# Loading, splitting and summing one half of the output's left operands from the fourth tile of mixer A's branch on

## The chip, the cores and the metric

The kernel runs on one core of a Trainium2 chip. The metric is the device time of one execution in microseconds (us), as the median of several runs. The engines are named PE (TensorE, matrix products), DVE (VectorE), ACT (ScalarE), POOL (GpSimd) and SP (SyncE, which here only issues transfers); PEld is the loading of weights into PE. A DMA is a transfer between the chip's memory and the core's SBUF.

## The reference

One layer of a decoder block on a sequence of 1024 rows and a width of 1024. Three branches (mixer A, a chunked spatial gating; mixer B, a windowed attention; mixer M, an attention into a memory) are each projected back to width 1024, summed under sigmoid gates, and multiplied by one output matrix:

```python
u = jax.nn.gelu(a_u, approximate=False)
vv = layer_norm(jax.nn.gelu(a_v, approximate=False), a_v_norm_w, a_v_norm_b)
y_a = chunked_spatial_gating(u, vv, a_spatial_w, a_spatial_b) * jax.nn.silu(a_z)
...
merged = (gates[:, :, 0] * (y_a @ proj_a)
          + gates[:, :, 1] * (y_b @ proj_b)
          + gates[:, :, 2] * (y_m @ proj_m))
x = x + merged @ w_out
```

The change touches how `merged @ w_out` is prepared while `y_a @ proj_a` is still being computed.

## The kernel before

**Number format.** A float32 operand is split into a high and a low part (`split`, L137 on ACT makes the high one, L138 on DVE the low one), and each product is three matrix products (`mm3`, L159 to L161). `piece` loads a weight (`ws_`, L142) and splits it into `wh_` and `wl_`.

**The stage around the change.** The last gating stage is mixer A's branch: `gates(0, w_pa, 6, yas, (0, 4, 1, 5, 2, 6, 3, 7), merged_done)`. It goes through eight tiles `dt` of the output's channels in that order, and each tile has two halves of 512 rows (tile 7 does its second half first). A half is one group of 18 matrix products (six weights of 128 columns, three products each) into one PSUM bank `pp`. PSUM has four banks of the tag `pj`, so the group that comes four later can only begin when DVE has read the bank at L1204 (`tg = (tg + 1) * pp`). Then POOL issues at L1206 a DMA that adds `tg` into `merged[dt]`; in tile 7 DVE adds it itself at L1208. The gate `tg` of a tile is loaded by SP at L1183 into one of three places.

**The output product** is done by a scheme of seven products over quadrants of the operands. Its right operands are `ro` (`right_sums`): for each pair of tiles `dt - 4` and `dt` it forms sums of quadrants of `merged` (L1301, L1305, L1306, L1307 on DVE) and splits each into two halves (`half_split`: L1288 on ACT, L1289 on DVE). L1301 needs both halves of `merged[dt - 4]` with the added `tg`, L1305 the second half of `merged[dt]`.

Its left operands are `left_o`, pieces of `w_out` for two column halves `c` and two row halves `kh`. For each (`c`, `kh`) `left_o_steps` gives the steps: "load" (four quadrants of 128x512), 1 to 7 (split for product 1 to 7), "sums" (L341 makes `so` from quadrants 21 and 22; L342 and L343 then combine quadrant 11 with them), and "last" (L346). The raw quadrants of `kh == 0` are in the weights' places `ws_o`, shared by all weights; those of `kh == 1` are in four places `wr_o` of their own (L1323).

**What sets the order.** The order in which the code is written is not that of the engines' queues: a scheduler lets the program's steps run ahead (so loads that the code asks for in tile 3 stand several tiles earlier on SP). Each engine runs its own queue strictly in order and stops at an instruction whose inputs aren't there.

After the stage, `partial(c, j, n, ks)` computes the products `po`, whose banks come from the same `pj` places (products 2 and 3 excepted); the first four begin with three of their four weights' tiles.

Of the kernel before, what the change touches and what calls it, by code (L numbers as in the profile page):

```python
# [41 lines left out]
def hybrid_block(  # L42
# [130 lines left out]
    last = [None]  # L173
# [156 lines left out]
    def prepare_left(load, extra, ready):  # L330


        w = {}

        def loads(*blocks):
            for b in blocks:
                w[b] = load((11, 21, 22, 12).index(b))

        def sums():
            w["s"] = extra()  # L340
            V.tensor_tensor(out=w["s"], in0=w[21], in1=w[22], op=ALU.add)  # L341
            V.tensor_tensor(out=w[21], in0=w[11], in1=w[21], op=ALU.subtract)  # L342
            V.tensor_tensor(out=w[11], in0=w["s"], in1=w[11], op=ALU.subtract)  # L343

        def last():
            V.tensor_tensor(out=w[12], in0=w[12], in1=w[11], op=ALU.subtract)  # L346

        return {"load": lambda: loads(11, 12, 21, 22), "11": lambda: loads(11), "12": lambda: loads(12),
                "2": lambda: loads(21, 22), "sums": sums, "last": last,
                1: lambda: ready(w[11], 1), 2: lambda: ready(w[12], 2), 3: lambda: ready(w[12], 3), 4: lambda: ready(w[22], 4), 5: lambda: ready(w["s"], 5),  # L350
                6: lambda: ready(w[11], 6), 7: lambda: ready(w[21], 7)}

# [22 lines left out]
    steps = deque()  # L375
# [7 lines left out]
    def ready(name):  # L383
        return lambda st, q: prepared.append(parts(st, 512, f"{name}_{q}"))
# [3 lines left out]
    def add_steps(ps_):  # L388


        def step(*keys):
            def run():
                for key in keys:
                    for p in ahead[nxt] if isinstance(key, tuple) and nxt < len(ahead) else ps_:
                        if not isinstance(key, tuple):
                            p[key]()
                        elif nxt < len(ahead):
                            for k in key if len(ahead[nxt]) == 2 else ("load",) * (key == ("2",)):
                                p[k]()
            return run  # L400

        n = len(ps_)
        ahead.append(ps_)
        nxt = len(ahead)
        steps.extend((n, step(*keys)) for keys in ((1,), (2,), ("sums", 6), (7, ("11",)), (5,), (4, ("12",)),
                                                   ("last", 3, ("2",))))

    tstack = ExitStack()
# [454 lines left out]
    with tc.tile_pool(name="npool", reuse_waits="tile", bufs=1, side="right") as npool:  # L863
# [55 lines left out]
        for b, targets in enumerate(naturals):  # L919
# [48 lines left out]
            for q in range(7):  # L968
                w = take(2)
                rh, rl = rights[q]  # L970
                for t in range(2):
# [13 lines left out]
                    n = len(later)  # L985
# [27 lines left out]
    with tc.tile_pool(name="ppool", reuse_waits="tile", bufs=1, side="right") as pp_:  # L1013
# [49 lines left out]
        for i, kind in enumerate(pairs):  # L1063
# [8 lines left out]
            for q in range(7):  # L1072
                p = 7 * i + q
# [210 lines left out]
    osteps = {}  # L1284
# [52 lines left out]
    def next_steps(c, n):  # L1337

        for p in osteps[c]:
            for key in ((1,), ("sums", 5), (2, "last", 3), (), (6,), (7,), (4,))[n]:  # L1340
                p[key]()

    def begin(c):
        osteps[c] = [left_o_steps(c, kh) for kh in range(2)]
        for p in osteps[c]:
            p["load"]()
        next_steps(c, 0)

    def merged_done(dt):
        right_sums(dt)  # L1350
        if dt == 3:
            begin(0)
            next_steps(0, 1)

    gates(0, w_pa, 6, yas, (0, 4, 1, 5, 2, 6, 3, 7), merged_done)
    next_steps(0, 2)
    late = deque(sorted(late, key=lambda t: PORDER.index(t[0])))
    jobs = [(0, j, n) for js in ((0, 1), (2, 3)) for ns in (range(2), range(2, 7)) for j in js for n in ns]
# [20 lines left out]
    for c, j, n in jobs:  # L1379
# [16 lines left out]
        if (c, j) == (0, 3):  # L1396
            if n == 0:
                begin(1)
            elif n != 2:
                next_steps(1, 2 if n == 3 else n)  # L1400

        def vadd(o, b=acc):
            V.tensor_tensor(out=o, in0=b, in1=o, op=ALU.add)
# [113 lines left out]
```

## Time and profile before

| what | value |
|---|---|
| three runs | 1119.02, 1120.58 and 1123.42 us |
| their median | 1120.58 us |
| the profiled execution's own time | 1120.26 us |
| the span of its trace | 1118.5 us |
| PE busy | 98 % of the span |
| DVE busy | 71 % |
| ACT busy | 46 % |
| POOL busy | 17 % |

The times in the rows below are microseconds from the beginning of the span of the profiled execution. Its own time, taken from outside, is 1.76 us longer than the span. The stage of mixer A's branch that the change touches runs from about 957 to 1024 us, and the output product follows it to the end.

### The profile page before, as it was taken

How to read it: one execution, taken by the hardware profiler on the slowest of the kernel's cores; microseconds unless marked ns; L12 is line 12 of the kernel's file. 1: busy time of each engine (PE TensorE's matmuls, PEld its weight loads, DVE VectorE, ACT ScalarE, POOL GpSimd, SP SyncE). 2: the span in 40 equal slices, each digit the busy share in tenths (PEclk: the TensorE clock that was granted, in tenths of full speed). 3: DMA queues.
4: the chain of work that ended last, by engine and by line, in shares of the span. 5: the costliest groups of instructions: out<-in, count | busy, mean ns of one | idle time of the engine just before them, and what ended most of it. 6: DMA issues, size and time to landing. Idle time of an engine off the chain costs nothing.

```text
span 1118.5 us, 18302 instructions
## 1 busy us (share of the span) xinstructions
PE 1092.7 (98%) x6680; PEld 955.9 (85%) x6680; DVE 794.1 (71%) x1701; ACT 514.0 (46%) x1123; POOL 195.7 (17%) x250
## 2 busy tenths in 40 slices
PE   8989999999999999999999999999999999998998
PEld 7879999999988887888888888888888787886998
DVE  6999899856687766656555656687885467568863
ACT  6553333223245543755665554666564562134320
POOL 0000431321000002011111111111111026511232
PEclk9999999999999999999999999999999999999999
DMA  7222322454242423444434325455544975665432
GB/s 236 76 96 91 128 86 96 144 190 151 72 142 94 129 98 119 143 147 153 128 121 136 124 95 181 123 180 157 166 132 132 335 273 160 173 161 136 142 107 83
DMA packets 84558, 157.57 MB, mean 141 GB/s; under 512 B 9605, under 2 KB 30708, under 8 KB 84468
## 3 DMA queue, kind: packets, MB, share of 16 engines
q1 hardware_dynamic: 68164, 106.87, 30.6%
q0 software_dynamic: 14864, 47.05, 13.0%
q10 hardware_dynamic: 1440, 2.49, 0.6%
q8 instruction: 52, 0.85, 0.3%
q14 instruction: 38, 0.31, 0.1%
HBM read 106.84 MB, written 48.22 MB: 139 GB/s over the span
## 4 chain that ended last, share of the span: by engine, by line
PE 86%; DVE 5%; DMA 4%; issue 3%; POOL 1%; ACT 1%; SPq 0%; POOLq 0%; DVEq 0%; ACTq 0%
PE t L159 12%; PE t L161 12%; PE t L160 11%; PE n L160 7%; PE n L159 7%; PE n L161 7%; PE po L606 3%; PE pp L159 2%; DMA merged<-tg 2%; PE pp L161 2%; PE pp L160 2%; PE po L160 2%; PE po L159 2%; PE po L161 2%; PE pt L599 1%
## 5 line engine op out<-in xcount | busy, mean ns | idle before, releaser
L159 PE MATMUL t<-th,wh_t 128*128 128x512 f32 x336 | 135.2, 402 | 0.0
L161 PE MATMUL t<-th,wl_t 128*128 128x512 f32 x336 | 132.0, 393 | 0.0
L160 PE MATMUL t<-tl,wh_t 128*128 128x512 f32 x336 | 131.4, 391 | 0.0
L159 PE MATMUL n<-wh_n,th 128*128 128x256 f32 x384 | 108.2, 282 | 0.0
L161 PE MATMUL n<-wh_n,tl 128*128 128x256 f32 x384 | 107.6, 280 | 0.0
L160 PE MATMUL n<-wl_n,th 128*128 128x256 f32 x384 | 107.6, 280 | 0.0
L161 PEld LDWEIGHTS t<-th,wl_t 128*128 128x128 f32 x336 | 63.1, 188 | 14.5
L159 PEld LDWEIGHTS n<-wh_n,th 128*128 128x128 f32 x384 | 73.3, 191 | 1.5 <-issue 0.9
L160 PEld LDWEIGHTS t<-tl,wh_t 128*128 128x128 f32 x336 | 63.3, 188 | 12.8
L159 PEld LDWEIGHTS t<-th,wh_t 128*128 128x128 f32 x336 | 63.3, 188 | 12.3
L160 PEld LDWEIGHTS n<-wl_n,th 128*128 128x128 f32 x384 | 72.1, 188 | 0.2 <-issue 0.2
L161 PEld LDWEIGHTS n<-wh_n,tl 128*128 128x128 f32 x384 | 72.2, 188 | 0.0
L159 PE MATMUL t<-H2h,wh_t 128*128 128x512 f32 x168 | 67.8, 404 | 0.0
L137 ACT CAST wh_t<-ws_t 128x512 fp32r<-128x512 f32 x86 | 51.8, 619 | 33.3 <-PE n L161 11.8
L161 PE MATMUL t<-H2h,wl_t 128*128 128x512 f32 x168 | 65.9, 392 | 0.0
L160 PE MATMUL t<-H2l,wh_t 128*128 128x512 f32 x168 | 65.5, 390 | 0.0
L138 DVE TENSOR_TENSOR wl_t<-ws_t,wh_t 128x512 fp32r<-128x512 f32 x86 | 58.2, 685 | 10.0 <-ACT wh_t L137 9.9
L1069 DVE TENSOR_TENSOR o<-t,sa 128x512 f32<-128x512 f32 x63 | 43.3, 687 | 29.5 <-PE t L161 25.1
L1038 POOL DMA_DIRECT2D scr_g<-o x48 | 26.1, 544 | 191.9 <-ACT o L1024 167.1
L939 POOL TENSOR_TENSOR on<-on,nss 128x1024 f32<-128x1024 f32 x12 | 26.2, 2205 | 173.4 <-DVE nss L134 116.0
L159 PE MATMUL n<-wh_n,H2h 128*128 128x256 f32 x192 | 54.9, 286 | 0.1
L160 PE MATMUL n<-wl_n,H2h 128*128 128x256 f32 x192 | 54.3, 283 | 0.0
(382 smaller groups left out, 3185.1 us busy)
## 6 DMA issues: line engine op xcount, KB each, us to landing
ws_t<-in_w_t SPq DMA_DIRECT2D x64, 256.0 KB, 3.5
scr_g<-o POOLq DMA_DIRECT2D x48, 256.0 KB, 2.7
tg<-scr_g SPq DMA_DIRECT2D x16, 512.0 KB, 3.9
ws_n<-in_w_n SPq DMA_DIRECT2D x24, 256.0 KB, 3.3
wr_n<-in_w_n SPq DMA_DIRECT2D x24, 256.0 KB, 3.3
scr_qk<-on POOLq DMA_DIRECT2D x12, 512.0 KB, 4.3
bx<-scr_qk SPq DMA_DIRECT2D x24, 256.0 KB, 3.3
wr_t<-in_w_t SPq DMA_DIRECT2D x20, 256.0 KB, 3.5
```

The lines of the kernel that those rows point to most:

```text
L137: A.copy(out=hi, in_=y)
L138: (eng or V).tensor_tensor(out=lo, in0=y, in1=hi.bitcast(F32), op=ALU.subtract)
L159: T.matmul(o, lhsT=ah, rhs=bh, start=first, stop=False)
L160: T.matmul(o, lhsT=ah, rhs=bl, start=False, stop=False)
L161: T.matmul(o, lhsT=al, rhs=bh, start=False, stop=last)
L599: T.transpose(p2[:, h * P:(h + 1) * P], c.pr[h // 2][:, h % 2, b * P:(b + 1) * P], ident)
L606: T.matmul(po[:, 64 * h:64 * h + 64], lhsT=c.pT[b][:, h * P:(h + 1) * P], rhs=mb.v[:, (t - nk + 1 + b) % 3, 64 * h:64 * h + 64], start=b = ...
L939: G.tensor_tensor(out=v, in0=v, in1=ss[:, 16 * ORD[q]:16 * ORD[q] + 16].unsqueeze(2) .to_broadcast([P, 16, 64]), op=ALU.mult)
L1038: G.dma_start(out=t[:, h], in_=d)
L1069: V.tensor_tensor(out=o[q], in0=psum, in1=s, op=ALU.add)
```

## The change

The combining steps of a left operand, which were one step "sums", become two: "s" (L341) and "rest" (L342 and L343, in the changed kernel L344 and L345). For the first column half (`c == 0`) the two row halves no longer go together: `kh == 1` is loaded and split for product 1 after the fourth tile (`dt == 5`) of mixer A's branch, gets its "s" and the split for product 5 after the fifth, and its "rest" after the sixth. `kh == 0` keeps its place after the seventh tile (`dt == 3`), but its "rest" comes behind the whole stage. For `c == 1` "rest" is done behind the split for product 5. The number of instructions stays the same. The lines behind L341 that the text names move down by two: L1204 is L1206 there, L1206 is L1208, L1288 and L1289 are L1290 and L1291, L1301 is L1303, L1305 to L1307 are L1307 to L1309, L1323 is L1325 and L346 is L348.

```diff
--- before.py
+++ after.py
@@ -336,9 +336,11 @@
             for b in blocks:
                 w[b] = load((11, 21, 22, 12).index(b))
 
-        def sums():
+        def first():
             w["s"] = extra()
             V.tensor_tensor(out=w["s"], in0=w[21], in1=w[22], op=ALU.add)
+
+        def rest():
             V.tensor_tensor(out=w[21], in0=w[11], in1=w[21], op=ALU.subtract)
             V.tensor_tensor(out=w[11], in0=w["s"], in1=w[11], op=ALU.subtract)
 
@@ -346,7 +348,7 @@
             V.tensor_tensor(out=w[12], in0=w[12], in1=w[11], op=ALU.subtract)
 
         return {"load": lambda: loads(11, 12, 21, 22), "11": lambda: loads(11), "12": lambda: loads(12),
-                "2": lambda: loads(21, 22), "sums": sums, "last": last,
+                "2": lambda: loads(21, 22), "s": first, "rest": rest, "last": last,
                 1: lambda: ready(w[11], 1), 2: lambda: ready(w[12], 2), 3: lambda: ready(w[12], 3), 4: lambda: ready(w[22], 4), 5: lambda: ready(w["s"], 5),
                 6: lambda: ready(w[11], 6), 7: lambda: ready(w[21], 7)}
 
@@ -402,7 +404,7 @@
         n = len(ps_)
         ahead.append(ps_)
         nxt = len(ahead)
-        steps.extend((n, step(*keys)) for keys in ((1,), (2,), ("sums", 6), (7, ("11",)), (5,), (4, ("12",)),
+        steps.extend((n, step(*keys)) for keys in ((1,), (2,), ("s", "rest", 6), (7, ("11",)), (5,), (4, ("12",)),
                                                    ("last", 3, ("2",))))
 
     tstack = ExitStack()
@@ -1337,7 +1339,7 @@
     def next_steps(c, n):
 
         for p in osteps[c]:
-            for key in ((1,), ("sums", 5), (2, "last", 3), (), (6,), (7,), (4,))[n]:
+            for key in ((1,), ("s", 5), (2, "last", 3), (), (6,), (7,), (4,))[n]:
                 p[key]()
 
     def begin(c):
@@ -1348,11 +1350,22 @@
 
     def merged_done(dt):
         right_sums(dt)
-        if dt == 3:
-            begin(0)
-            next_steps(0, 1)
+
+        if dt == 5:
+            osteps[0] = [left_o_steps(0, kh) for kh in range(2)]
+            osteps[0][1]["load"]()
+            osteps[0][1][1]()
+        elif dt == 2:
+            osteps[0][1]["s"]()
+            osteps[0][1][5]()
+        elif dt == 6:
+            osteps[0][1]["rest"]()
+        elif dt == 3:
+            for key in ("load", 1, "s", 5):
+                osteps[0][0][key]()
 
     gates(0, w_pa, 6, yas, (0, 4, 1, 5, 2, 6, 3, 7), merged_done)
+    osteps[0][0]["rest"]()
     next_steps(0, 2)
     late = deque(sorted(late, key=lambda t: PORDER.index(t[0])))
     jobs = [(0, j, n) for js in ((0, 1), (2, 3)) for ns in (range(2), range(2, 7)) for j in js for n in ns]
@@ -1398,6 +1411,9 @@
                 begin(1)
             elif n != 2:
                 next_steps(1, 2 if n == 3 else n)
+                if n == 1:
+                    for p in osteps[1]:
+                        p["rest"]()
 
         def vadd(o, b=acc):
             V.tensor_tensor(out=o, in0=b, in1=o, op=ALU.add)
```

What the scheduler makes of it is seen in the engines' queues. PE's and POOL's order stays as it was. In the rows a name's number tells one tile from another.

**DVE at the stage's first two tiles.** `tg_10127` is the gate of tile 0, `tg_10141` that of tile 4, `merged_9367` is `merged[0]`. Before:

```order
L1204 SCALAR_TENSOR_TENSOR tg_10127<-tg_10127,pp_10155 128x512
L138 TENSOR_TENSOR wl_p_10345<-ws_p_10342,wh_p_10344 128x256
L1204 SCALAR_TENSOR_TENSOR tg_10127<-tg_10127,pp_10176 128x512
L1289 SCALAR_TENSOR_TENSOR ro_10253<-merged_9367,ro_10253 128x512
L138 TENSOR_TENSOR wl_p_10420<-ws_p_10417,wh_p_10419 128x512
L1301 TENSOR_TENSOR merged_9367<-merged_9367 128x512
L1204 SCALAR_TENSOR_TENSOR tg_10141<-tg_10141,pp_10211 128x512
```

With the change (`wr_o_10419` and `wr_o_10421` are quadrants 21 and 22 of `kh == 1`, `wr_o_10415` is quadrant 11):

```order
L1206 SCALAR_TENSOR_TENSOR tg_10127<-tg_10127,pp_10155 128x512
L341 TENSOR_TENSOR so_10483<-wr_o_10419,wr_o_10421 128x512
L138 TENSOR_TENSOR wl_p_10345<-ws_p_10342,wh_p_10344 128x256
L344 TENSOR_TENSOR wr_o_10419<-wr_o_10415,wr_o_10419 128x512
L1206 SCALAR_TENSOR_TENSOR tg_10127<-tg_10127,pp_10176 128x512
L1291 SCALAR_TENSOR_TENSOR ro_10253<-merged_9367,ro_10253 128x512
L138 TENSOR_TENSOR wl_o_10424<-wr_o_10415,wh_o_10423 128x512
L345 TENSOR_TENSOR wr_o_10415<-so_10483,wr_o_10415 128x512
L1303 TENSOR_TENSOR merged_9367<-merged_9367 128x512
L1206 SCALAR_TENSOR_TENSOR tg_10141<-tg_10141,pp_10211 128x512
```

Three instructions that need the loads of `kh == 1` (L341, L344 and, behind the second half, L345 with a split) now stand ahead of the sum L1301 (now L1303), two of them ahead of the second half's L1204 (now L1206). One split of a weight, `wl_p` 128x512, has moved behind it.

**SP, the loads of the same stretch.** `tg_10141` and `tg_10197` are the gates of tiles 4 and 1. Before:

```order
L1183 DMA tg_10141<-scr_g_651 128x1024
L1323 DMA wr_o_10607<-in_w_o 128x512
L1323 DMA wr_o_10609<-in_w_o 128x512
L1183 DMA tg_10197<-scr_g_648 128x1024
L142 DMA ws_p_10473<-in_w_pa 128x512
L1323 DMA wr_o_10611<-in_w_o 128x512
L1323 DMA wr_o_10613<-in_w_o 128x512
L142 DMA ws_p_10479<-in_w_pa 128x256
```

With the change:

```order
L1185 DMA tg_10141<-scr_g_651 128x1024
L1325 DMA wr_o_10415<-in_w_o 128x512
L1325 DMA wr_o_10417<-in_w_o 128x512
L1185 DMA tg_10197<-scr_g_648 128x1024
L1325 DMA wr_o_10419<-in_w_o 128x512
L1325 DMA wr_o_10421<-in_w_o 128x512
L142 DMA ws_p_10491<-in_w_pa 128x512
```

The second pair of loads of `kh == 1`, quadrants 21 and 22, moves ahead of one weight load of 128x512.

**DVE at the sixth tile.** `tg_10415` (before) and `tg_10427` (after) are the gate of tile 6, `merged_9369` is `merged[2]`. Before:

```order
L1289 SCALAR_TENSOR_TENSOR ro_10527<-merged_9369,ro_10527 128x512
L138 TENSOR_TENSOR wl_o_10620<-wr_o_10607,wh_o_10619 128x512
L138 TENSOR_TENSOR wl_o_10628<-so_10623,wh_o_10627 128x512
L342 TENSOR_TENSOR wr_o_10611<-wr_o_10607,wr_o_10611 128x512
L1204 SCALAR_TENSOR_TENSOR tg_10415<-tg_10415,pp_10485 128x512
L1301 TENSOR_TENSOR merged_9369<-merged_9369 128x512
L343 TENSOR_TENSOR wr_o_10607<-so_10631,wr_o_10607 128x512
L1289 SCALAR_TENSOR_TENSOR ro_10531<-merged_9369,ro_10531 128x512
L138 TENSOR_TENSOR wl_o_10636<-so_10631,wh_o_10635 128x512
L1204 SCALAR_TENSOR_TENSOR tg_10415<-tg_10415,pp_10506 128x512
```

With the change:

```order
L1291 SCALAR_TENSOR_TENSOR ro_10545<-merged_9369,ro_10545 128x512
L138 TENSOR_TENSOR wl_p_10574<-ws_p_10571,wh_p_10573 128x256
L138 TENSOR_TENSOR wl_o_10628<-ws_o_10619,wh_o_10627 128x512
L1303 TENSOR_TENSOR merged_9369<-merged_9369 128x512
L1206 SCALAR_TENSOR_TENSOR tg_10427<-tg_10427,pp_10503 128x512
L341 TENSOR_TENSOR so_10631<-ws_o_10623,ws_o_10625 128x512
L1291 SCALAR_TENSOR_TENSOR ro_10549<-merged_9369,ro_10549 128x512
L344 TENSOR_TENSOR ws_o_10623<-ws_o_10619,ws_o_10623 128x512
L345 TENSOR_TENSOR ws_o_10619<-so_10631,ws_o_10619 128x512
L138 TENSOR_TENSOR wl_o_10634<-so_10631,wh_o_10633 128x512
L1206 SCALAR_TENSOR_TENSOR tg_10427<-tg_10427,pp_10524 128x512
```

Before, the first half's L1204 stood ahead of the sum L1301, and three instructions lay between that sum and the second half's L1204. Now both halves' gates stand behind the sum (L1303), with five further instructions between them: L341, L344, L345 and a split of `kh == 0` (`so_10631`) have come here, and those of `kh == 1` that stood ahead of tile 6 (L138 twice, L342) have left.

## Rows read from the trace of the kernel before

**Rows 1.** Page, part 1: busy us (share of the span) and instructions.

```profile
PE 1092.7 (98%) x6680; PEld 955.9 (85%) x6680; DVE 794.1 (71%) x1701; ACT 514.0 (46%) x1123; POOL 195.7 (17%) x250
```

**Rows 2.** Windows: length, busy PE, PEld, DVE, ACT, POOL, clock, DMA share, GB/s.

```profile
1020.00:1040.00 20.00, 14.84 (x84) 13.80 (x83) 17.57 (x29) 10.64 (x20) 1.69 (x2) 0.83 0.52 133
```

**Rows 3.** PE's waits, 960 to 1118 us: in total, times, longest.

```profile
PE po L159 <- DVE tg L1204: 5.2, 2, 2.9
...
PE pp L159 <- DVE tg L1204: 0.3, 1, 0.3
```

**Rows 4.** PE's timeline behind the first stall: start, duration.

```profile
1027.43 0.41 PE L160 MATMUL po<-wl_o,ro 128*128 128x256 f32 x1
1027.65 0.41 PE L161 MATMUL po<-wh_o,ro 128*128 128x256 f32 x1
...
1030.50 0.28 PE L160 MATMUL po<-wl_o,ro 128*128 128x256 f32 x1
1030.62 0.28 PE L161 MATMUL po<-wh_o,ro 128*128 128x256 f32 x1
```

**Rows 5.** PE's timeline: first products of tile 5 and of tile 2's second half.

```profile
981.82 0.39 PE L159 MATMUL pp<-ya,wh_p 128*128 128x512 f32 x1
...
994.18 0.39 PE L159 MATMUL pp<-ya,wh_p 128*128 128x512 f32 x1
```

**Rows 6.** DVE's timeline, tiles 0 and 4: start, duration, idle before and its releaser.

```profile
967.22 0.68 DVE L1204 SCALAR_TENSOR_TENSOR tg<-tg,pp 128x512 f32<-128x512 f32 x1
974.42 0.69 DVE L1289 SCALAR_TENSOR_TENSOR ro<-merged,ro 128x512 fp32r<-128x512 f32 x1 [6.53 <-ACT ro L1288]
...
977.98 0.69 DVE L1301 TENSOR_TENSOR merged<-merged 128x512 f32<-128x512 f32 x1 [2.27 <-DMA merged<-tg]
...
980.32 0.68 DVE L1204 SCALAR_TENSOR_TENSOR tg<-tg,pp 128x512 f32<-128x512 f32 x1
...
986.24 0.69 DVE L1305 TENSOR_TENSOR merged<-merged,merged 128x512 f32<-128x512 f32 x1 [4.64 <-DMA merged<-tg]
```

**Rows 7.** Chain that ended last, 930 to 1060 us: start, us, what.

```profile
968.20 9.69 DMA merged<-tg
...
981.29 4.93 DMA merged<-tg
...
1011.35 3.29 DMA merged<-tg
```

**Rows 8.** Windows, columns as in rows 2.

```profile
970.00:974.00 4.00, 4.00 (x19) 3.30 (x18) 0.00 (x0) 0.25 (x1) 0.00 (x0) 1.00 1.00 259
```

**Rows 9.** SP's timeline: the second pair of loads of `wr_o`.

```profile
967.89 0.96 SPq L1323 DMA_DIRECT2D wr_o<-in_w_o  x2
```

**Rows 10.** Tile `wr_o`: landing of the pair issued from 963.2, then from 967.9.

```profile
DMA to landing us min/median/max: 3.9/4.0/4.1
...
DMA to landing us min/median/max: 6.6/7.2/7.7
```

**Rows 11.** DVE's timeline, from tile 2 to the stage's last gate.

```profile
1002.64 0.69 DVE L341 TENSOR_TENSOR so<-ws_o,ws_o 128x512 f32<-128x512 f32 x1 [1.51 <-DMA ws_o<-in_w_o]
1003.25 0.68 DVE L341 TENSOR_TENSOR so<-wr_o,wr_o 128x512 f32<-128x512 f32 x1
...
1006.16 0.68 DVE L1204 SCALAR_TENSOR_TENSOR tg<-tg,pp 128x512 f32<-128x512 f32 x1
...
1013.58 0.68 DVE L1204 SCALAR_TENSOR_TENSOR tg<-tg,pp 128x512 f32<-128x512 f32 x1
1014.73 0.69 DVE L1301 TENSOR_TENSOR merged<-merged 128x512 f32<-128x512 f32 x1 [0.46 <-DMA merged<-tg]
...
1017.39 0.68 DVE L1204 SCALAR_TENSOR_TENSOR tg<-tg,pp 128x512 f32<-128x512 f32 x1
...
1021.91 0.69 DVE L1305 TENSOR_TENSOR merged<-merged,merged 128x512 f32<-128x512 f32 x1 [2.52 <-DMA merged<-tg]
...
1033.03 0.68 DVE L1204 SCALAR_TENSOR_TENSOR tg<-tg,pp 128x512 f32<-128x512 f32 x1
```

## Prediction

> **What bounds the kernel now.** First the page's busy shares: PE is busy for 98 % of the span and DVE for 71 % [rows 1], so only PE's idle time can be won, and the question is where PE waits around the change. PE's list of waits from 960 us on gives that: 5.2 us in two waits of a first product `po` for L1204, the longer 2.9 and so the other 2.3, and 0.3 us in one wait of a gating group `pp` for the same line [rows 3]. So PE walks through mixer A's branch almost undisturbed and pays at its end, in the stretch 1020 to 1040, where it is busy for 14.84 of 20 us at a mean granted clock of 0.83 [rows 2]. The clock is part of that price. Behind the first stall the products start 0.22 us apart (1027.43, 1027.65) at half the rate, and 0.12 apart by 1030.50 (to 1030.62) [rows 4], which are the two levels of 1.2 and 2.4 GHz; some 15 products pass at the slow one, 15 x 0.10 = 1.5 us. The second stall follows the same pattern, so both together cost at most 5.2 + 2 x 1.5 = 8.2 us. That is the most that any better order of DVE's queue in this stage can win.
>
> Then DVE's timeline says why L1204 is late. The last one starts at 1033.03 [rows 11], though PE ended its third partial product at 1030.62 + 0.28 = 1030.90 [rows 4]. DVE isn't short of capacity: it stands still for 6.53 us ahead of the split of `merged[0]`, then 2.27 us ahead of L1301, 4.64 us ahead of L1305 [rows 6] and 2.52 us ahead of the last L1305 but one [rows 11], each time until an accumulating DMA `merged<-tg` has landed. Every L1204 behind such a sum waits in DVE's queue with it, and issues its own accumulating DMA the later: a chain gate, DMA, sum, next gate. The chain of waits shows it: 9.69 us of landing from 968.20, 4.93 from 981.29, later 3.29 from 1011.35 [rows 7]. What is worth something here is therefore the place of a step relative to these waits. DVE's work as such is covered by them.
>
> **The change part by part.**
>
> *Number of steps.* Nothing is added or removed: as many loads, splits and sums as before, 0.60 us of DVE each (two L341 start at 1002.64 and 1003.25 [rows 11]). The split of "sums" into two costs nothing by itself. Taking steps away ahead of tile 2 is worth little: what leaves there (two L341, L342, two splits) stood ahead of an L1305 that was held by its DMA.
>
> *Early place: a wait is added in front of a gate.* In the new order L341 of `kh == 1` stands directly behind the first half's gate of tile 0, and behind it in the queue wait a weight's split, L344 and the second half's gate. L341 needs quadrants 21 and 22. Their loads are issued from 967.89 [rows 9] and in the kernel before land 6.6 and 7.7 us later [rows 10], at 967.9 + 6.6 = 974.5 and 968.4 + 7.7 = 976.1. They move ahead of one load of 256 KB, so the later one now takes about the place of the earlier: 974.5 is my value, 976.1 the upper bound, and the lower 972.4 if they land in the 4.0 us of the pair issued at 963 [rows 10]. The stretch 970 to 974 has all 16 DMA engines busy [rows 8], which is why I stay near the long landing. From there: L341 0.60, the 128x256 split 0.35, L344 0.60, so the second half's gate starts at 974.5 + 1.55 = 976.05 instead of 967.22 [rows 6]. PE doesn't need it before tile 1's second group, one group ahead of the one at 981.82; three groups lie between that and 994.18 [rows 5], 4.12 us each, so at 977.7: covered, with 1.0 us to spare.
>
> Its accumulating DMA however starts as much later: 0.98 us behind the gate (967.22 to 968.20 [rows 6, 7]), so at 977.0. Its landing I take as 3.3 to 3.6 us (the row of 1011.35 and the like [rows 7]), since the loads it had fought with have landed by then; as long as before, 9.7 us, is the upper bound. It lands at 980.3 to 980.6, and the sum L1301 moves from 977.98 [rows 6] to about 980.5, by +2.5; with loads at 972.4 it would be +0.4. Tile 4's first gate is then done at 980.5 + 1.3 = 981.8, and PE wants it for tile 5 at 981.82 [rows 5]: no stall to speak of. The second half's gate of tile 4 was at 980.32 [rows 6] and moves to 982.5 or so, because one 128x512 split less lies ahead of it. Its DMA landed in 4.93 us [rows 7]; with 3.6 to 4.9 the next sum, L1305, moves from 986.24 [rows 6] by +0.9 to +2.2. From here on the order is nearly the old one (a split of `so` comes into tile 1, one split of a right operand leaves tile 2), and the delay is handed on, less what it finds of idle DVE: 2.29 us ahead of the next L1301 were also a wait in this same chain and give nothing back. At tile 2's first gate, 1006.16 before [rows 11], I expect +0.1 to +2.3, and take +1.2. PE may stall by up to 1.5 us at 994.18 [rows 5]; that stall adds nothing, since PE waits anyway at the end.
>
> *Late place: `kh == 0` at tile 6.* Between tile 2's first gate and the last gate lie 1033.03 - 1006.16 = 26.87 us [rows 11]. L343 (0.6) leaves that stretch and one split of a right operand (0.6) enters it. At tile 6 the first gate now stands behind the sum L1301, and behind it five steps instead of three. Before: sum at 1014.73, second gate at 1017.39, 2.66 us apart [rows 11]. Now: sum, gate, five steps, 7 x 0.60 = 4.2 us. That is +1.54. The DMA of that gate is awaited by the next L1305, which stood idle for 2.52 us until it landed [rows 11]; nothing hides the delay, and it goes on to the last gate. The "rest" of `kh == 0`, now behind the stage, needs 1.2 us before products 6 and 7 want it, many products later: covered; without cover, 1.2 us.
>
> *Sum.* +1.2 (early) + 1.5 (late) = +2.7 us on the last gate, for which PE already waits, so the end moves by the same: 1120.26 + 2.7 = 1123.0 us. The profiled execution is 0.3 us under the median of the runs shown, so the median would be some 1123.2; I write 1123.0. From the bounds: -0.5 (the early part gives 0.1, and a right operand's split that now stands behind tile 2's first gate instead of ahead of it wins 0.6) to +2.3 + 1.8 (three more steps of 0.60, with no wait saved) + 1.5 (a third spell of slow clock, if a stall inside the stage brings one) = +5.6.
>
> The Trainium skill, page "DMA: Bandwidth & Descriptors", section "Issuing engines are not separate DMA queues", says that transfers started by different engines run on the same 16 engines and interleave. By that rule the accumulating DMA, now started behind the loads, would share with fewer of them; the trace agrees so far as the 9.7 us landing falls into the stretch with a DMA share of 1.00 [rows 7, 8].
>
> **Rivals.**
>
> *A, no change.* The loads land as fast as the pair issued at 963, in 4 us [rows 10], so L341 stops the queue only to 972.4. Then the second gate is at 974, its DMA lands by 978.5, and the early term is 0 to +0.4; the late term may be smaller if its sum isn't DMA-bound any more. Time: 1120.3 to 1122. For it: the two pairs have the same size. Against it: the DMA engines were full in the very stretch [rows 8], and the second pair took 6.6 and 7.7 us there [rows 10]. [...]
>
> *B, faster.* The steps of `kh == 1` now run in waits of 6.5 and 2.3 us in which DVE did nothing [rows 6], and the late stretch holds fewer. If the last gate comes before 1030.9, when PE ends its third partial product [rows 4], the second stall and its slow clock vanish: -2.9 - 1.5 = -4.4 us, 1115.9; with the first stall gone as well up to -8.2, 1112.1. For it: the idle time is there. Against it: what ends the wait is a DMA that itself starts later, and the step nearest the end gets more in front of it. It decides from a last gate 2.1 us earlier than now.
>
> *C, clearly slower.* The late accumulating DMA meets the weight loads that have moved behind it, and lands in 9.7 us again: sum at 977.0 + 9.7 = 986.7, tile 4's first gate done at 988. PE stands at 981.82 [rows 5] for 6 us with a slow spell behind it. The stage has little slack left, so 6 to 9 us reach the end: 1126 to 1129. It decides from a landing of more than about 6 us. For it: the row of 9.69 [rows 7]. Against it: the later two of the same size took 4.93 and 3.29 [rows 7].
>
> *D, nothing moves*, since the scheduler could undo it: excluded by the queues' order.
>
> **How the numbers follow.** The likeliest case (chance 0.50) is 1121.5 to 1125.9, A 0.22, C 0.18, B 0.10 (two thirds of it over 0.5 % faster). Half a per cent, 5.6 us, is about what a measurement of this kernel tells from no change: 1115.0 to 1126.2. Faster: 0.08. Slower: most of C and the upper edge of the likeliest, 0.18. Same: 0.74. The range leaves out B's larger half and C's upper end: 1116.5 to 1128.
>
> **What would show it.** In the changed trace: L341 of `wr_o` waits for a DMA ahead of the second gate of tile 0, some 5 us, and that gate starts near 976; its DMA lands in under 5 us; L1303 of `merged[0]` starts near 980.5; the distance from L1303 of `merged[2]` to the second gate of tile 6 is 4.2 us; the last gate starts near 1035.7 and the two `po` stalls are longer by the same. I am wrong if L341 waits for nothing, if L1303 comes after 984, or if the last gate isn't DMA-bound and comes earlier than 1031.

## The result, and the profile after

| what | before | changed |
|---|---|---|
| median of six runs each | 1119.93 us | 1126.54 us |
| lowest and highest | 1119.02, 1123.42 us | 1124.93, 1130.36 us |
| the profiled execution's own time | 1120.26 us | 1124.93 us |
| the span of its trace | 1118.5 us | 1123.2 us |

The changed kernel takes 1.0061 times as long, with a 95 % interval of 1.0044 to 1.0078. The profiled execution of the changed kernel is the quickest of its six; against the one before it lost 4.7 us, and that is what the rows below can explain. The medians lie 6.6 us apart; the 1.9 us more are in no trace.

DVE's timeline of the changed kernel (start, duration, idle before and its releaser) answers to [rows 6] and [rows 11]; L1206 is the gate that was L1204, L1303 and L1307 are the sums that were L1301 and L1305:

```profile
965.98 0.68 DVE L1206 SCALAR_TENSOR_TENSOR tg<-tg,pp 128x512 f32<-128x512 f32 x1
974.89 0.69 DVE L341 TENSOR_TENSOR so<-wr_o,wr_o 128x512 f32<-128x512 f32 x1 [8.23 <-DMA wr_o<-in_w_o]
...
976.43 0.68 DVE L1206 SCALAR_TENSOR_TENSOR tg<-tg,pp 128x512 f32<-128x512 f32 x1
...
980.76 0.69 DVE L1303 TENSOR_TENSOR merged<-merged 128x512 f32<-128x512 f32 x1 [1.71 <-DMA merged<-tg]
...
988.67 0.69 DVE L1307 TENSOR_TENSOR merged<-merged,merged 128x512 f32<-128x512 f32 x1 [4.30 <-DMA merged<-tg]
...
1008.78 0.68 DVE L1206 SCALAR_TENSOR_TENSOR tg<-tg,pp 128x512 f32<-128x512 f32 x1
...
1017.83 0.69 DVE L1303 TENSOR_TENSOR merged<-merged 128x512 f32<-128x512 f32 x1 [1.83 <-DMA merged<-tg]
1018.44 0.68 DVE L1206 SCALAR_TENSOR_TENSOR tg<-tg,pp 128x512 f32<-128x512 f32 x1
...
1022.18 0.68 DVE L1206 SCALAR_TENSOR_TENSOR tg<-tg,pp 128x512 f32<-128x512 f32 x1
...
1037.89 0.68 DVE L1206 SCALAR_TENSOR_TENSOR tg<-tg,pp 128x512 f32<-128x512 f32 x1
```

L341 stops DVE for 8.23 us until its load has landed, with the second half's gate of tile 0 behind it: 976.43 against 967.22 [rows 6]. The first sum comes at 980.76 instead of 977.98, the next at 988.67 instead of 986.24 [rows 6], tile 2's first gate at 1008.78 instead of 1006.16 [rows 11]. At tile 6 it is 4.35 us from the sum (1017.83) to the second gate (1022.18), before 2.66 [rows 11]. The last gate is at 1037.89, before at 1033.03 [rows 11].

The landing of tile `wr_o`'s second pair of loads, and of the accumulating DMA of tile 0's second half (issued at 977.42), answer to [rows 10] and to the 9.69 us of [rows 7]:

```profile
DMA to landing us min/median/max: 5.4/6.1/6.7
...
DMA to landing us min/median/max: 3.3/3.3/3.3
```

PE's waits from 960 us on (in total, times, longest), to [rows 3], and the window 1020 to 1040, to [rows 2]:

```profile
PE po L159 <- DVE tg L1206: 6.0, 4, 2.6
PE pp L159 <- DVE tg L1206: 2.2, 2, 1.4
...
PE pp L159 <- ACT ro L1290: 0.8, 1, 0.8
```

```profile
1020.00:1040.00 20.00, 14.00 (x67) 11.61 (x66) 16.82 (x28) 8.40 (x16) 3.03 (x4) 0.83 0.53 128
```

PE waits only 0.8 us more at the end (6.0 against 5.2), but 3.0 us inside the stage (2.2 and 0.8) where it had waited 0.3. The lateness shows there first: PE's first product of the output starts at 1023.57 before and at 1028.14 with the change, so nearly all of the 4.7 us has arisen by then.

```profile
1023.57 0.28 PE L159 MATMUL po<-wh_o,ro 128*128 128x256 f32 x1
...
1028.14 0.36 PE L159 MATMUL po<-wh_o,ro 128*128 128x256 f32 x1 [0.39 <-DVE tg L1206]
```

The waits inside the stage bring no slow clock with them: in both of its windows the changed kernel's granted clock (the third number from the end) is 1.00.

```profile
980.00:1000.00 20.00, 19.20 (x83) 15.23 (x82) 12.50 (x21) 5.93 (x11) 4.22 (x5) 1.00 0.61 143
1000.00:1020.00 20.00, 17.71 (x75) 13.66 (x74) 12.68 (x22) 6.64 (x13) 2.88 (x4) 1.00 0.64 158
```

### The profile page after: what moved, and what is told of

It is laid out like the page before. It is cut to its first block, busy times and chain, and to the rows that moved or that the text cites. A ratio compares the mean times of both kernels' runs of the same rounds, so it can differ in the third digit from the quotient of the medians.

```text
span 1123.2 us, 18308 instructions
## 1 busy us (share of the span) xinstructions
PE 1094.5 (97%) x6680; PEld 955.9 (85%) x6680; DVE 793.3 (71%) x1701; ACT 513.8 (46%) x1123; POOL 195.8 (17%) x250
## 5 line engine op out<-in xcount | busy, mean ns | idle before, releaser
L138 DVE TENSOR_TENSOR wl_t<-ws_t,wh_t 128x512 fp32r<-128x512 f32 x86 | 58.2, 685 | 9.3 <-ACT wh_t L137 9.2
```

The lines of the kernel that those rows point to most:

```text
L138: (eng or V).tensor_tensor(out=lo, in0=y, in1=hi.bitcast(F32), op=ALU.subtract)
```

## The experiments

The executions enter the stage at different times (tile 0's first gate, 965.78 before, is at 965.0 to 968.4 in the others), so stage times are counted from that gate. The first numeric column is the ratio to the kernel before with its 95 % interval, then come the time to tile 2's first gate, to the last gate, and to the end of the span, each from one trace.

| kernel | ratio to before | tile 2's gate | last gate | end |
|---|---|---|---|---|
| before | 1 | 40.38 | 67.25 | 152.7 |
| changed | 1.0061 (1.0044 to 1.0078) | 42.80 | 71.91 | 157.2 |
| e1, sums of `kh == 1` behind the gate | 1.0021 (1.0006 to 1.0035) | 40.25 | 70.14 | 155.5 |
| e2, loads of `kh == 1` earlier | 1.0029 (1.0016 to 1.0042) | 40.44 | 70.64 | 155.9 |
| e3, steps of `kh == 1` asked for later | 1.0045 (1.0027 to 1.0062) | 44.41 | 72.41 | 157.7 |
| e4, e1 and e3 | 1.0022 (1.0009 to 1.0036) | 41.95 | 70.25 | 155.6 |
| e5, steps of `kh == 0` behind tile 6's gate | 1.0046 (1.0030 to 1.0061) | 43.16 | 72.12 | 157.4 |
| e6, e1 and e5 | 1.0025 (1.0013 to 1.0037) | 39.92 | 69.01 | 154.3 |
| e7, before, last gate ahead | 1.0001 (0.9989 to 1.0012) | 39.77 | 65.59 | 152.2 |
| e8, e6 and e7 | 1.0028 (1.0017 to 1.0039) | 40.76 | 68.25 | 154.9 |
| e9, e1 and early splits undone | 0.9994 (0.9979 to 1.0009) | 40.03 | 66.45 | 152.0 |
| e10, `kh == 1` at its old place | 0.9997 (0.9983 to 1.0011) | 41.19 | 68.17 | 153.5 |
| e11, before, second halves added by DVE | 0.9967 (0.9954 to 0.9980) | 37.93 | 63.89 | 148.9 |
| e12, changed, second halves added by DVE | 0.9975 (0.9963 to 0.9987) | 40.22 | 64.83 | 149.9 |

e7's queues are those of the kernel before up to tile 3, and e10's hardly differ from them, so 39.8 to 41.2 in the column of tile 2's gate, and about 1 us of the next, is what one trace scatters against another.

**e1: the sums behind the gate.** An edge for the order of issue alone, with no wait in it, queues DVE's steps behind a gate (`gate` keeps the instruction of L1206 of each tile and half):

```diff
         elif dt == 2:
-            osteps[0][1]["s"]()
+            with tc.issue_after(gate[0, 0, 1]):
+                osteps[0][1]["s"]()
             osteps[0][1][5]()
         elif dt == 6:
-            osteps[0][1]["rest"]()
+            with tc.issue_after(gate[0, 0, 1]):
+                osteps[0][1]["rest"]()
```

> The changed kernel with one thing undone on DVE: the sum L341 and L344 of kh == 1 are queued behind the second half's gate of tile 0 instead of ahead of it; all loads stay as in the changed kernel. Theory (the wait of L341 in front of that gate delays the chain gate, accumulating DMA, sum): the gate is back near 967, the sum of merged[0] near 978 to 978.6, everything after it 2 to 2.7 us earlier than in the changed kernel, so the last gate near 1035.3 and the time some 2.5 us under the changed kernel's, about 1122 to 1124. Rival (the loads that moved on SP, and their traffic, are what costs): the gate is early but the sums and the time stay where the changed kernel has them.

DVE's timeline of e1, the two gates of tile 0, the first sum (L1305 here), tile 2's first gate and the last:

```profile
967.44 0.68 DVE L1208 SCALAR_TENSOR_TENSOR tg<-tg,pp 128x512 f32<-128x512 f32 x1
...
968.88 0.68 DVE L1208 SCALAR_TENSOR_TENSOR tg<-tg,pp 128x512 f32<-128x512 f32 x1
...
979.98 0.68 DVE L1305 TENSOR_TENSOR merged<-merged 128x512 f32<-128x512 f32 x1
...
1007.69 0.68 DVE L1208 SCALAR_TENSOR_TENSOR tg<-tg,pp 128x512 f32<-128x512 f32 x1
...
1037.58 0.68 DVE L1208 SCALAR_TENSOR_TENSOR tg<-tg,pp 128x512 f32<-128x512 f32 x1
```

The second gate is 1.44 us behind the first again, and tile 2's gate is at 40.25, where it was before (40.38). The whole early delay of 2.4 us is gone with two instructions moved and every load left where the change had put it. The median is 1123.69 us, 2.9 under the changed kernel's, and the two ratios' intervals don't meet. So the wait ahead of the gate is shown as the cause of the early term; the rival of the moved loads falls for this term. The last gate gains only 1.8 us (70.14 against 71.91) where 2 to 2.7 had been forecast: from tile 2's first gate on, e1 loses 3.0 us against the kernel before.

**e2: the loads earlier.** The loads of `kh == 1` are asked for ahead of `gates(0, ...)`:

```diff
         if dt == 5:
-            osteps[0] = [left_o_steps(0, kh) for kh in range(2)]
-            osteps[0][1]["load"]()
             osteps[0][1][1]()
...
+    osteps[0] = [left_o_steps(0, kh) for kh in range(2)]
+    osteps[0][1]["load"]()
     gates(0, w_pa, 6, yas, (0, 4, 1, 5, 2, 6, 3, 7), merged_done)
```

> The changed kernel with the four loads of kh == 1 asked for ahead of the stage: on SP the second pair now stands directly behind the first, ahead of the gate load of tile 1; on DVE L341 is still ahead of the second half's gate. Theory (only the lateness of the loads matters, not the place as such): the second pair is issued near 964.5 instead of 967.6 and lands by 970; L341 waits until then, the gate starts near 971.5 and the time lies between the changed kernel's and that of the run with the sums held, 1 to 2.5 us under the changed kernel's. Rival (the order on DVE itself, whatever the loads do): as the changed kernel.

DVE's timeline of e2:

```profile
969.66 0.69 DVE L341 TENSOR_TENSOR so<-wr_o,wr_o 128x512 f32<-128x512 f32 x1 [3.99 <-DMA wr_o<-in_w_o]
...
971.33 0.68 DVE L1206 SCALAR_TENSOR_TENSOR tg<-tg,pp 128x512 f32<-128x512 f32 x1
...
1005.44 0.68 DVE L1206 SCALAR_TENSOR_TENSOR tg<-tg,pp 128x512 f32<-128x512 f32 x1
```

The landing of the accumulating DMA behind that second gate, issued at 972.32:

```profile
DMA to landing us min/median/max: 4.8/4.8/4.8
```

L341 still stands ahead of the gate and waits 3.99 us, but with its loads landed at 969.7 the delay no longer reaches tile 2's gate (40.44). Place and lateness both matter: a gate 6.3 us behind the first costs nothing there, one 10.5 us behind it (the changed kernel's) costs 2.4 us. Before, the gate was 1.4 us behind the first. What takes up e2's 4.9 us is the landing of its accumulating DMA, 4.8 us where it had been 9.7 [rows 7]; with the change it falls to 3.3 us, and 9.0 us of delay are more than that saves. The Trainium skill, page "DMA: Bandwidth & Descriptors", section "Rules for kernel authors", advises to issue a DMA early and wait on it late; e1 (wait later) and e2 (issue earlier) each agree with it, with the numbers above.

**e3 and e4: the late place, by asking later.** The steps "s", 5 and "rest" of `kh == 1` are called in `dt == 3`; e4 has e1's edge as well.

```diff
-        elif dt == 2:
-            osteps[0][1]["s"]()
-            osteps[0][1][5]()
-        elif dt == 6:
-            osteps[0][1]["rest"]()
         elif dt == 3:
+            for key in ("s", 5, "rest"):
+                osteps[0][1][key]()
             for key in ("load", 1, "s", 5):
```

> The changed kernel with the steps s, rest and 5 of kh == 1 asked for after the seventh tile: on DVE the early place is as in the changed kernel (L341 waits in front of the gate of tile 0), but at tile 6 the combining steps of kh == 0 stand ahead of the sum again, and two instructions instead of five lie between that sum and the second gate. Theory (two separate terms): the early delay of 2.6 us stays, the late one of 1.7 to 2.2 us goes; last gate near 1035.5 to 1036, time 1.5 to 2.2 us under the changed kernel's. Rival (the late order is covered by the wait for the DMA): time as the changed kernel.

> Both edits together: sums of kh == 1 behind the gate of tile 0, and the late steps ahead of the sum at tile 6. Theory (the two terms add up to the whole loss): last gate at 1032.5 to 1033.5, time as the kernel before within 1 us. Rival (a further cost, such as the moved loads or the stalls within the stage): 2 us or more over the kernel before.

DVE's timeline of e3, from tile 2's second gate on:

```profile
1016.58 0.68 DVE L1206 SCALAR_TENSOR_TENSOR tg<-tg,pp 128x512 f32<-128x512 f32 x1
...
1020.87 0.69 DVE L1303 TENSOR_TENSOR merged<-merged 128x512 f32<-128x512 f32 x1 [0.47 <-DMA merged<-tg]
...
1023.53 0.68 DVE L1206 SCALAR_TENSOR_TENSOR tg<-tg,pp 128x512 f32<-128x512 f32 x1
```

From the sum to the second gate of tile 6 it is 2.66 us again, as before. But the last gate of e3 is at 72.41, no earlier than in the changed kernel. The steps taken away there stand between tile 2's two gates now (5.41 us apart, before 4.21 in DVE's timeline), and tile 2's first gate is itself 1.6 us later than in the changed kernel: 0.9 us of that lie ahead of tile 5's second gate, and the last accumulating DMA ahead of tile 2 landed in 5.7 us, in the changed kernel in 5.0. e4 recovers what e1 does and no more (1.0022). Expectation missed: the two terms don't add.

**e5 and e6: the late place, hidden behind the gate.** The steps "s", 5 and "rest" of `kh == 0` are queued behind the second half's gate of tile 6; e6 has e1's edge as well.

```diff
         elif dt == 3:
-            for key in ("load", 1, "s", 5):
+            for key in ("load", 1):
                 osteps[0][0][key]()
+            with tc.issue_after(gate[0, 6, 1]):
+                for key in ("s", 5):
+                    osteps[0][0][key]()
...
-    osteps[0][0]["rest"]()
+    with tc.issue_after(gate[0, 6, 1]):
+        osteps[0][0]["rest"]()
```

> The changed kernel with the steps s, 5 and rest of kh == 0 queued on DVE behind the second half's gate of tile 6, where DVE otherwise waits 2.5 us for that gate's accumulating DMA; the early place is as in the changed kernel. Theory (what stands between the sum and the gate of tile 6 is paid in full, what stands behind the gate is hidden): from the sum to that gate 2.0 us instead of 4.35, from tile 2's first gate to the last gate 26.8 us instead of 29.1; the early 2.5 us stay; time some 2.3 us under the changed kernel's. Rival (these steps cost DVE time wherever they stand, as in the run that moved them ahead of the sum): 29.1 us, time as the changed kernel.

> The changed kernel with both sets of steps behind the gates: L341 and L344 of kh == 1 behind the second half's gate of tile 0, those of kh == 0 behind that of tile 6; loads as in the changed kernel. Theory (two waits and nothing else make the loss): from the first gate of tile 0 to the last gate 67.5 to 68 us (before 67.25, changed 71.91), time within 1 us of the kernel before. Rival (the moved loads cost on their own, through the landing of the accumulating DMAs): 69 us or more, time 2 us over the kernel before.

DVE's timeline of e6 at tile 6 (L1305 is the sum) and its last gate, and the load of `kh == 0` that SP issues ahead of it:

```profile
1013.06 0.42 DVE L138 TENSOR_TENSOR wl_p<-ws_p,wh_p 128x256 fp32r<-128x256 f32 x1
...
1017.21 0.69 DVE L1305 TENSOR_TENSOR merged<-merged 128x512 f32<-128x512 f32 x1 [3.13 <-DMA merged<-tg]
...
1019.27 0.68 DVE L1208 SCALAR_TENSOR_TENSOR tg<-tg,pp 128x512 f32<-128x512 f32 x1
...
1036.42 0.68 DVE L1208 SCALAR_TENSOR_TENSOR tg<-tg,pp 128x512 f32<-128x512 f32 x1
```

```profile
1013.50 0.33 SPq L142 DMA_DIRECT2D ws_o<-in_w_o  x1
```

The distance from the sum to the gate is 2.06 us, as the theory said, yet from tile 2's first gate to the last gate it is 29.09 us in e6 and 28.96 in e5, hardly less than the changed kernel's 29.11. The sum is later instead, by 1.0 us: its accumulating DMA, issued at 1012.8, lands in 4.3 us where it took 3.3, and a load of `kh == 0` of the same size goes out at 1013.50, right behind it. And from tile 6's second gate to the last one it takes 17.15 us, before 15.64: one more split stands ahead of tile 7's first gate (0.8 us), and the last accumulating DMA lands in 4.7 us instead of 3.3. So what was put behind the gate was not all hidden either. The time stays 0.25 % over before (e6). Here my theory of two terms fell, and the rival held: something else that came with the change costs about 2.5 us.

**e7 and e8: the last gate ahead.** On the kernel before, and on e6, the last tile's sums and the splits for later products are queued behind the last gate.

```diff
-        right_sums(dt)
+        if dt == 7:
+            with tc.issue_after(gate[0, 7, 0]):
+                right_sums(dt)
+        else:
+            right_sums(dt)
...
-                next_steps(0, done)
+                with tc.issue_after(gate[0, 7, 0]):
+                    next_steps(0, done)
...
-            right_late(1)
+            with tc.issue_after(gate[0, 7, 0]):
+                right_late(1)
```

> The kernel before with one thing moved: on DVE the sums and splits of the last tile's right operands, and the left and right splits of the products behind it, stand behind the last gate instead of ahead of it. Theory (PE pays at the stage's end for the last gate's place in DVE's queue): the last gate comes at 29.5 to 30 instead of 33.0 counted from 1000 us, PE's second stall of 2.9 us vanishes with its slow clock, and some of it returns as a wait for the splits that now come later: 2 to 4 us faster than before. Rival (DVE is the bound behind the stage, so a later split takes the stall's place): within 1 us of before.

> The changed kernel with all three edits: both sets of steps behind their gates and the last gate ahead of the last tile's sums. Theory: as the kernel before with the last gate moved, 2 to 4 us faster than before, 8 to 10 us faster than the changed kernel. Rival (the parts do not add): no faster than the run with both sets of steps held.

PE's waits of e7:

```profile
PE po L159 <- DVE tg L1206: 3.5, 2, 1.9
PE po L159 <- ACT sm L1420: 1.3, 1, 1.3
PE po L159 <- ACT ro L1290: 1.2, 1, 1.2
PE po L159 <- DVE xr L1411: 0.7, 1, 0.7
```

The waits for the gates shrink from 5.2 [rows 3] to 3.5 us, and PE waits 3.2 us instead for what now comes later, where the kernel before had waited 1.6 us for ACT and DVE. No gain (1.0001), and none on top of e6 (1.0028): both theories missed, and e7's last gate came 1.7 us earlier, not 3 or more. Taking a step out of a gate's way pays only if the step has somewhere to go.

**e9: the early splits undone.** e1, e6 and e8 all split `kh == 1` early for products 1 and 5; e3 and e4 do so for product 1 alone. `parts` puts a split into two of the nine places `wh` and `wl`, which the weights of mixer A's branch share. The weights' last split, L138 into `wl_p` of 128x256, stands in DVE's timeline at 998.90 before, and at 1014.98 in the changed kernel; SP's last load of `kh == 0` goes out right behind it, at 999.35 before, and at 1015.42 in the changed kernel:

```profile
998.90 0.42 DVE L138 TENSOR_TENSOR wl_p<-ws_p,wh_p 128x256 fp32r<-128x256 f32 x1
...
999.35 0.33 SPq L142 DMA_DIRECT2D ws_o<-in_w_o  x1
```

```profile
1014.98 0.42 DVE L138 TENSOR_TENSOR wl_p<-ws_p,wh_p 128x256 fp32r<-128x256 f32 x1
...
1015.42 0.33 SPq L142 DMA_DIRECT2D ws_o<-in_w_o  x1
```

So e9 keeps the early loads and e1's edge for "s", and puts splits 1 and 5 and "rest" of `kh == 1` into `dt == 3`:

```diff
             osteps[0][1]["load"]()
-            osteps[0][1][1]()
         elif dt == 2:
-            osteps[0][1]["s"]()
-            osteps[0][1][5]()
-        elif dt == 6:
-            osteps[0][1]["rest"]()
+            with tc.issue_after(gate[0, 0, 1]):
+                osteps[0][1]["s"]()
         elif dt == 3:
+            for key in (1, 5, "rest"):
+                osteps[0][1][key]()
             for key in ("load", 1, "s", 5):
```

> The changed kernel with L341 and L344 of kh == 1 behind the second half's gate of tile 0, and the splits of kh == 1 for products 1 and 5 asked for only after the seventh tile; the loads of kh == 1 stay early. New theory (the late term and what was left over in the run with both sets held come from these two early splits: they keep two of the nine places wh and wl, so the weights of the last two tiles are split later, their raw places come free later, and the loads of kh == 0 start later and fall on the accumulating DMAs): the weights' last split is back near tile 5, the loads of kh == 0 are issued some 10 us earlier, from tile 2's first gate to the last gate 26 to 27 us, time within 1 us of the kernel before. Rival (the early loads or sums alone cost the 2.5 us): time 2 us or more over the kernel before.

e9's DVE and SP timelines:

```profile
999.66 0.42 DVE L138 TENSOR_TENSOR wl_p<-ws_p,wh_p 128x256 fp32r<-128x256 f32 x1
...
1006.75 0.68 DVE L1208 SCALAR_TENSOR_TENSOR tg<-tg,pp 128x512 f32<-128x512 f32 x1
...
1033.17 0.68 DVE L1208 SCALAR_TENSOR_TENSOR tg<-tg,pp 128x512 f32<-128x512 f32 x1
```

```profile
991.14 3.93 SPq L142 DMA_DIRECT2D ws_o<-in_w_o  x2
...
1000.11 0.33 SPq L142 DMA_DIRECT2D ws_o<-in_w_o  x1
```

The last weight is split at 999.66, the last load of `kh == 0` goes out 15 us earlier than in the changed kernel, from tile 2's first gate to the last it takes 26.42 us, and the time is that of the kernel before (0.9994). None of the loss is left, though the loads and L341 and L344 of `kh == 1` stay early. The order at tile 6 is nearly that of before as well (2.66 us from the sum to the second gate), but e3 to e6 had shown that this alone returns nothing.

e4 narrows it further. Of what e9 makes late, only the split for product 1 and L345 of `kh == 1` are early there, and a loss of 0.22 % stays, so both splits are not needed for it. The last weight is then split 35.7 us behind the first gate (before 33.1, changed 49.0) and the last load of `kh == 0` goes out at 36.2 (before 33.6, changed 49.4): little lateness suffices, and in e4 L341 and L344 of `kh == 0` come to stand between tile 2's gates. That the splits act through the places, and by no other effect of asking for them early, is argued and not shown; a kernel with more places was not run.

**e10: one part alone.** The kernel before with the sums divided and `kh == 0`'s "rest" behind the stage; the change's new order for `c == 1` stays in it too:

```diff
         if dt == 3:
             begin(0)
-            next_steps(0, 1)
+            osteps[0][0]["s"]()
+            osteps[0][0][5]()
+            for key in ("s", "rest", 5):
+                osteps[0][1][key]()
 
     gates(0, w_pa, 6, yas, (0, 4, 1, 5, 2, 6, 3, 7), merged_done)
+    osteps[0][0]["rest"]()
```

> One part alone: the kernel before with the sums split into two steps, and the rest of kh == 0 behind the whole stage; kh == 1 at its old place. Every theory so far: as the kernel before, within 1 us, first gate of tile 0 to last gate 66.5 to 67.5 us. Rival (putting the rest of kh == 0 behind the stage makes products 6 or 7 wait): some 1 us slower, with a wait of PE on a split of a left operand.

As before (0.9997). This part of the change costs nothing, as forecast. Its one profiled trace is 0.9 us late at the last gate (68.17, outside the 66.5 to 67.5 that I had expected); the accumulating DMA ahead of tile 2's first gate had landed in 5.0 us, before in 4.4.

**e11 and e12: the chain cut.** The second halves of tiles 0 to 6 are added into `merged` by DVE, in the kernel before and in the changed one:

```diff
-                if br == 0 and dt < 7:
+                if br == 0 and dt < 7 and i == 0:
                     G.dma_start(out=m, in_=tg[:, t], accum_op=ALU.add)
```

> The kernel before, with the second halves of tiles 0 to 6 added into merged by DVE (0.6 us each) instead of by the accumulating DMA. Theory (the stage is a chain gate, accumulating DMA, sum, gate; the DMA's 4.3 to 10 us on it are what makes the gates late): DVE hardly waits in the stage, the last gate follows PE's last group, comes 4 us or more earlier than 67.25 us behind the first gate, PE's stalls of 2.3 and 2.9 us shrink; 2 to 7 us faster than before. Rival (DVE's work is the bound, and 7 more operations add to it): 0 to 4 us slower.

> The changed kernel with the same second halves added by DVE. Theory (the change costs because it lengthens a chain through accumulating DMAs): with the chain cut the wait of L341 is caught up with by the end of the stage, and the time is within 1.5 us of the kernel before with the same edit. Rival (the change costs by itself): 4 to 6 us slower than the kernel before with the same edit.

DVE's waits of the kernel before, 965 to 1040 us, then those of e11 and e12:

```profile
DVE merged L1305 <- DMA merged<-tg: 7.5, 3, 4.6
...
DVE merged L1301 <- DMA merged<-tg: 5.4, 4, 2.3
```

```profile
DVE ro L1289 <- ACT ro L1288: 15.0, 7, 6.4
```

```profile
DVE so L341 <- DMA wr_o<-in_w_o: 8.5, 1, 8.5
DVE ro L1291 <- ACT ro L1290: 8.1, 5, 4.8
```

No sum waits for an accumulating DMA any more. The last gate comes 3.4 us earlier (63.89 against 67.25), and e11 is 0.33 % faster than before, the interval clear of 1, though DVE has seven operations more. Two parts of the theory were missed: the gain at the last gate is under the 4 us forecast, and DVE still waits 15.0 us for ACT's half of the splits (L1288). ACT in its turn waits for the first halves' accumulating DMAs, which e11 leaves:

```profile
ACT ro L1288 <- DMA merged<-tg: 25.1, 6, 9.3
```

So the chain is cut at the sums only. In e12 the wait of L341 is as long as ever, 8.5 us, and costs next to nothing: 1117.05 us in the median, the same as e11. By the ratios e12 is 0.08 % behind e11, with intervals that overlap, where the change had cost 0.61 %; in the one trace of each the last gate is 0.9 us later. So nearly all of what the change costs goes through the sums' waits for the second halves' DMAs; a small rest isn't excluded. e11 and e12 beat both kernels.

## Why the prediction was right, and where it was off

The time fell into the range and moved as forecast, but by 4.7 us in the profiled execution instead of 2.7. The ratio of 0.61 % is over the line of 0.5 %, to which I had given 0.18 against 0.74 for no change.

That it fell into the range was in part luck. The median, 1126.54 us, lies above the likeliest case's 1125.9; the range reaches to 1128 only for rival C, which didn't happen. The last gate moved by 4.86 us, inside the sum's +5.6, but both of its parts passed their upper bounds (2.6 against 2.3, 2.2 against 1.8), and the 1.5 us for a third spell of slow clock, which made room for them, was not needed: PE did stall inside the stage, at a granted clock of 1.00.

*The wait ahead of the gate.* Right in place and size. Each time the forecast stands first and the measured value second: L341 released at 974.5 and 974.89; gate at 976.05 and 976.43; its accumulating DMA issued at 977.0 and 977.42, landing in 3.3 to 3.6 and in 3.3; sum at 980.5 and 980.76. Only the wait's duration was wrong in the list of what to look for: 8.23 us, not 5, since it begins right behind the first gate. Rival A, loads landing in 4 us, falls: 5.4 and 6.7. Rival C, a second slow landing, falls too.

*What of it reaches tile 2's gate.* The step that failed is "handed on, less what it finds of idle DVE", with the +1.2 taken from it between +0.1 and +2.3. Measured +2.6, or +2.4 counted from the first gate: just over the upper end. The idle time that was to soften it belongs to the same chain: each wait ends with a DMA that starts later by about the same amount, so 2.8 at the first sum, 2.4 at the second and 2.6 at tile 2's gate. One reading of the order was wrong besides: tile 4's second gate came at 983.36 and not at 982.5, because the split of 128x512 that no longer stood ahead of the sum stood ahead of this gate. e1 shows that all of it is this one wait.

*The late place.* The step at tile 6 was forecast as +1.54 and measured as 4.35 - 2.66 = 1.69. From tile 2's first gate to the last it is +2.24 in all: 0.31 more lies between tile 2's gates, and 0.17 in the landing at the sum of tile 6. So the size at tile 6 was near, but as the cause of the loss the step failed, and that its 1.5 us came so near is luck: with the order undone the loss stays (e3 to e6). By e9 and e4 the cause lies with the early splits. Their consequence includes loads of `kh == 0` that go out some 10 to 16 us later (1002.07 for 990.43, 1015.42 for 999.35), beside accumulating DMAs. The one ahead of tile 2's first gate landed in 5.0 us instead of 4.4, but it took 5.0 in e10 as well, so that one shows nothing; the clear cases are those of e6, 4.3 and 4.7 us instead of 3.3. I had costed the moved loads at tile 0 and not those that the scheduler then put elsewhere.

*Where PE pays.* Forecast: the two `po` stalls grow by the same. Measured: they grow by 0.8 us, and 2.7 us more are waited for inside the stage. So the way was another than forecast: PE arrives late at the output product rather than waiting longer there. The end moves with the last gate all the same, 85.5 us behind it before (1118.5 - 1033.03) and 85.3 with the change (1123.2 - 1037.89).

*Rival B, the gain.* Its idle time was real, but only e11 shows a way to have some of it: by shortening the chain, not by filling its waits.

## What to carry to other kernels

Before an instruction is moved ahead, look at what stands behind it in its engine's queue: a side task that waits for a load in front of the instruction that starts the next transfer of a chain delays the whole chain, however idle the engine is. A wait that ends with a DMA which the same queue started is no safe slack: a delay ahead of it starts the DMA later and is handed on, unless the DMA then lands faster (e2's 4.9 us were taken up that way, the changed kernel's 9.0 us left 2.4). And an early step that takes a shared place can push out what would have used it (here argued from e9 and e4); follow the places, and the loads that they hold up, as well as the instructions.

## What was not expected of the hardware

An accumulating DMA of 256 KB from POOL landed in 3.2 to 3.3 us in six of its 14 uses in the kernel before. In e6 two of them had a load of 256 KB issued 0.66 and 0.56 us behind them and landed in 4.3 and 4.7 us; the same two took 3.3 us in the kernel before, where no load followed so closely. That of tile 0's second half took 9.0 to 9.9 us in all kernels that issue it at 968 to 971, 4.8 us when issued at 972.32 (e2) and 3.3 us at 977.42 (the changed kernel). The same addition costs DVE 0.6 us. In a chain, seven such additions on DVE, the busier engine, were cheaper than seven DMAs started by POOL, by 3.4 us at the last gate.
